# The weight sum S1 of each Strassen group: added by an accumulating DMA of GpSimd's queue instead of by VectorE

## The chip, the cores and the metric

The kernel runs on one core of a Trainium2 chip. The metric is the device time of one execution in microseconds (us). The engines are PE (TensorE, matrix products), DVE (VectorE), ACT (ScalarE), POOL (GpSimd) and SP (SyncE, which here only issues transfers). Every engine works through its own list of instructions in order and waits on semaphores for the others.

## The reference

One block of an encoder in float32, 1024 tokens of width 1024: two SwiGLU feed-forward layers around a token mixing stage.

```
h = h + 0.5 * swiglu_ffn(rmsnorm(h), ffn1_w_in, ffn1_w_out)
u = rmsnorm(h); proj = u @ w_in          # q, k, v, g_ret, p, gates
...                                       # retention, multi-scale pooling
merged = gate0 * (ret @ w_ret_up) + gate1 * (pool_out @ w_pool_up)
h = h + merged @ w_out
h = h + 0.5 * swiglu_ffn(rmsnorm(h), ffn2_w_in, ffn2_w_out)
return rmsnorm(h)

swiglu_ffn(x) = (silu(gate) * up) @ w_out,  [gate | up] = x @ w_in
```

The feed-forward width is 2816, and w_in has 7168 columns.

## The kernel before, in words

Activations are held transposed, channels on the partitions and tokens along the free dimension. Each product of a weight with activations is worked out in float32 from two parts of each operand, a rounded high part and the rest: `split` (L150 to L152) makes them, the high part by a cast on ACT (L151), the low part by a subtraction on DVE (L152), and `mm3` (L171 to L173) does three matmuls of 512 columns for each product.

The large weight matrices go through Strassen's scheme in Winograd's form: seven products of blocks instead of eight. One *group* is `strassen()` (L391): it takes two adjacent tiles of 128 output channels, wa and wb, each 128 x 1024, and cuts each in two halves of 512: L11 and L12 from wa, L21 and L22 from wb. The weight side of the scheme is S1 = L21 + L22, S2 = S1 − L11, S3 = L11 − L21, S4 = L12 − S2. `blocks()` in it loads wa to a tile `ra` and wb to `rb` (two loads of 512 KB on SP's queue, `load`, L134) and `combine()` (L403 to L405) makes each sum on DVE, one instruction of 128 x 512. In the order of the code S1 is made just ahead of S2, in the step of S2, and read again later, when the step of S1 splits it for its own product.

Each of the seven steps has a preparation (`prep_w`: sums, then the split) and a body (`b1` to `b7`: 12 matmuls on PE, then copies and evacuations). `b1` begins a bank for the sum b by copying the first product on ACT (L437, "a_b" from "a_a" in the profile); the next product of b goes onto that copy, so PE needs it. `Flow.run` calls the preparation of a step four steps (`LOOK`) ahead of its body. Background work (evacuating, scaling, storing of earlier groups) is added between bodies, some pieces a step (`flow.rate`). Evacuations marked `soon` get a high priority from the scheduler of the tile framework, which sets the order on each engine and puts in the waits.

Buffers come from pools: `raw` (4 tiles of 128 x 1024, for ra and rb), `wt` (5, split weights) and `c2` (8 tiles of 128 x 512; S1 to S4 and most intermediate values of an evacuation). A new tile in a pool waits until the last reader of the tile that it replaces is done.

79 groups use `strassen()`: 21 in the first feed-forward's input (names a1 to a21, one more, a0, is done plainly), 28 in the projections (v, t, g, p, q, k), 8 in the merge (ru0 to ru3 and wo0 to wo3), 22 in the second feed-forward's input (c0 to c21). In the feed-forwards gate tiles g and up tiles g + 11 take turns: a11, a1, a12, a2 and so on, and two groups that follow each other form a pair (a16 and a6, then a17 and a7). In most pairs the seventh product is shared: `third()` gives both groups' S4 terms from one product's worth of smaller ones, so a pair takes 13 products. When a gate tile and its up tile are done and the swish is taken, `w1`, `w2`, `w3` in `ffn_in` store the operands for the next stage: b, r, t and m, four stores on SP's queue (m is made by the subtraction at L669). The output products of the feed-forwards (`ffn_out`) have their own S1, S2, S3; the change does not touch those.

Of the kernel before, what the change touches and what calls it, by code (L numbers as in the profile page):

```python
# [15 lines left out]
ADD, SUB, MUL = ALU.add, ALU.subtract, ALU.mult  # L16
# [5 lines left out]
H = S // 2  # L22
# [67 lines left out]
def block_kernel(ctx: ExitStack, tc, x, x_tok, vecs, f1_in, f1_out, w_in, pool_w, w_ret, w_pool, w_o,  # L90
                 f2_in, f2_out, rope, decay, consts, out, out_tok):
    nc = tc.nc
# [21 lines left out]
    def raw(name):  # L114
        return sb.tile([P, S], F32, tag="raw", bufs=N_RAW, name=name)
# [7 lines left out]
    def c2(name):  # L123
        return sb.tile([P, H], F32, tag="c2", bufs=N_C2, name=name)

    def bank(name):
        return ps.tile([P, H], F32, tag="ps", name=name)

    def sum_bank(name):

        return ps.tile([P, H], F32, tag="sum", bufs=N_SUM, name=name)

    def load(dst, src):
        nc.sync.dma_start(dst, src)  # L134
# [4 lines left out]
    def half(t, j):  # L139
        return t[:, j * H : (j + 1) * H]  # L140
# [22 lines left out]
    def weights(src, name):  # L163
        w = wt(name)
        n = src.shape[-1] // P
        split(flat(w, 0, n), flat(w, 1, n), src)
        return w

    def mm3(dst, w, m, start, stop):

        mm(dst, w[0], m[0], start=start, stop=False, skip_group_check=True)  # L171
        mm(dst, w[0], m[1], start=False, stop=False, skip_group_check=True)  # L172
        mm(dst, w[1], m[0], start=False, stop=stop, skip_group_check=True)  # L173

    def parts(m, at=slice(None)):
        return m[:, 0, at], m[:, 1, at]
# [214 lines left out]
    def strassen(nx, wa, wb, name, evac, end, begin=None, shared=False):  # L391

        t = {}

        def blocks():
            ra, rb = raw(f"{name}ra"), raw(f"{name}rb")
            load(ra, wa)
            load(rb, wb)  # L400
            t.update(L11=half(ra, 0), L12=half(ra, 1), L21=half(rb, 0), L22=half(rb, 1))

        def combine(n, a, b, op):  # L403
            t[n] = c2(f"{name}{n}")
            tt(t[n], t[a], t[b], op)  # L405

        def prep_w(n):
            def go():
                if n == "L11":
                    blocks()  # L410
                elif n == "S2":
                    combine("S1", "L21", "L22", ADD)
                    combine("S2", "S1", "L11", SUB)
                elif n == "S3":
                    combine("S3", "L11", "L21", SUB)
                if n == "S4" or shared and n == "L22":
                    combine("S4", "L12", "S2", SUB)
                t["w", n] = weights(t[n], f"{name}w{n}")

            return go  # L420

        def prod(dst, w, m, start, stop):
            for i in range(4):
                mm3(t[dst], parts(t["w", w], i), parts(nx.operand(m, i)), start and i == 0, stop and i == 3)

        def u(n):
            t[n] = c2(f"{name}{n}")
            return t[n]

        def b1():  # L430
            if begin:
                begin()
            t["a"] = bank(f"{name}a")
            prod("a", "L11", "R11", True, False)
            t["b"] = sum_bank(f"{name}b")
            with soon():
                copy(t["b"], t["a"])  # L437

        def b6():
            prod("b", "S2", "T2", False, False)  # L440
            with soon():
                copy(u("v"), t["b"])

        def fourth():

            if "b5" in t and "p7" in t:
                with soon():
                    evac((1, 1), t["b"], t["p7"])

        def b5():  # L450
            prod("b", "S1", "T1", False, False)
            t["b5"] = True
            fourth()

        def b7():
            t["e"] = bank(f"{name}e")
            prod("e", "S3", "T3", True, False)
            with soon():
                copy(u("p7"), t["e"])
            fourth()  # L460

        def b2():
            prod("a", "L12", "R21", False, True)
            with soon():
                evac((0, 0), t["a"], None)

        def b3():
            prod("b", "S4", "R22", False, True)
            with soon():
                evac((0, 1), t["b"], None)  # L470

        def b4():
            prod("e", "L22", "T4", False, True)
            with soon():
                evac((1, 0), t["e"], t["v"])

        def last(f):
            def go():
                f()
                t["ends"] = t.get("ends", 0) + 1  # L480
                if t["ends"] == 2:
                    end()

            return go

        g = Group([(prep_w("L11"), b1), (prep_w("S2"), b6), (prep_w("S1"), b5), (prep_w("S3"), b7),
                   (prep_w("L12"), b2), (prep_w("S4"), last(b3)), (prep_w("L22"), last(b4))])
        g.t, g.name, g.third = t, name, last(lambda: evac((0, 1), t["b"], t.get("z")))
        return g
# [965 lines left out]
    class Last(Norm):  # L1455
# [58 lines left out]
        def end(self, part):  # L1514
            if part == 2:
                flow.add(self.finish)
                return
            tokens = (slice(H, S), slice(0, HD))[part]
            at = {}

            def stats():
                r = inverse_root(token_sums(self.ssq, range(tokens.start // P, tokens.stop // P), f"fin{part}"), D,
                                 f"fin{part}")
                at["b"] = spread(r, f"fin{part}")

            def scale(mt):
                t = self.tiles[mt][:, tokens]
                stt(t, t, vec[:, V_FINAL + mt : V_FINAL + mt + 1], at["b"], MUL, MUL)
                load(out[mt, :, tokens], t)

            flow.add(stats, *(lambda mt=mt: scale(mt) for mt in range(KT)))
            if part == 1:
                flow.add(*(lambda mt=mt: self.gain(mt) for mt in range(4)))
# [94 lines left out]
```

## Time and profile before

| | |
|---|---|
| median of 3 runs | 2176.23 us (2175.84 to 2177.58) |
| profiled execution | 2176.49 us |
| its span | 2174.3 us |
| mean granted clock | 0.998 |
| transfers | 311.96 MB, 143 GB/s over the span |

The page of the profile gives each engine's busy time, the chain of work that ended last, and groups of instructions. Names leave out buffer numbers: "a_S" is S1, S2, S3 or S4 of some a group, "a_rb" its rb tile, "a_wS" a split of such a sum. A row of a timeline has the start, the length, the engine (SPq is the queue of SP), the line, the operation, and in brackets the idle time ahead of it with what ended it. Lines of DMA issues end with the median time from issue to landing.

### The profile page before, as it was taken

The numbers are of one execution on the slowest core, as the hardware profiler recorded it, in microseconds if no ns is written. First come the engines' busy times: TensorE is split into PE (matmuls) and PEld (weight loads), VectorE is DVE, ScalarE is ACT, GpSimd is POOL, SyncE is SP. The second block draws the span as 40 slices with busy tenths as digits, with TensorE's granted clock in tenths as the row PEclk, the third lists the DMA queues.
The fourth block names the chain that finished last, engine by engine and source line by source line (L and its number), as shares of the span: only waits on it lengthen the run. The fifth ranks groups of instructions, "written<-read, shape, count | busy, mean of one in ns | idle before, by whom it ended". The sixth has DMA issues, their size and how long they took to land.

```text
span 2174.3 us, 29003 instructions
## 1 busy us (share of the span) xinstructions
PE 2163.3 (99%) x10556; PEld 1825.3 (84%) x10556; DVE 1786.0 (82%) x3068; ACT 1041.0 (48%) x1911; POOL 0.2 (0%) x4
## 2 busy tenths in 40 slices
PE   9999999999999999999999999999999999999998
PEld 7888888888888888888888998878888888888888
DVE  8797878888687687888887787799997878799774
ACT  8443434455554434444446663456634434344561
POOL 0000000000000000000000000000000000000000
PEclk9999999999999999999999999999999999999999
DMA  6233323596323332323345557524232322359522
GB/s 231 86 125 110 126 92 106 181 329 218 101 92 114 110 136 97 126 97 124 109 175 184 187 188 276 188 88 142 82 136 83 126 93 93 125 186 342 174 83 78
DMA packets 110448, 311.96 MB, mean 143 GB/s; under 512 B 12385, under 2 KB 13537, under 8 KB 110305
## 3 DMA queue, kind: packets, MB, share of 16 engines
q1 hardware_dynamic: 110304, 310.11, 41.4%
q8 instruction: 83, 1.36, 0.3%
q14 instruction: 61, 0.49, 0.1%
HBM read 219.36 MB, written 90.70 MB: 143 GB/s over the span
## 4 chain that ended last, share of the span: by engine, by line
PE 96%; DVE 2%; ACT 1%; DMA 0%; issue 0%; SPq 0%; DVEq 0%; ACTq 0%
PE c_b L171 2%; PE c_b L173 2%; PE c_b L172 2%; PE a_b L172 2%; PE a_b L171 2%; PE a_b L173 2%; PE c_e L171 2%; PE c_a L172 2%; PE c_a L171 2%; PE c_a L173 2%; PE c_e L173 2%; PE c_e L172 2%; PE a_a L172 2%; PE a_a L171 2%; PE a_e L172 2%; PE a_e L171 2%
## 5 line engine op out<-in xcount | busy, mean ns | idle before, releaser
L151 ACT CAST c_wS<-c_S 128x512 fp32r<-128x512 f32 x72 | 44.7, 621 | 74.9 <-DVE c_S L405 47.6
L172 PE MATMUL c_a<-n3R,c_wL 128*128 128x512 f32 x176 | 68.7, 390 | 0.0
L173 PE MATMUL c_a<-n3R,c_wL 128*128 128x512 f32 x176 | 68.5, 389 | 0.0
L172 PE MATMUL c_b<-n3T,c_wS 128*128 128x512 f32 x176 | 68.5, 389 | 0.0
L173 PE MATMUL c_b<-n3T,c_wS 128*128 128x512 f32 x176 | 68.5, 389 | 0.0
L171 PE MATMUL c_a<-n3R,c_wL 128*128 128x512 f32 x176 | 68.4, 390 | 0.0
L171 PE MATMUL c_b<-n3T,c_wS 128*128 128x512 f32 x176 | 68.1, 389 | 0.0
L151 ACT CAST a_wS<-a_S 128x512 fp32r<-128x512 f32 x68 | 42.1, 620 | 52.3 <-DVE a_S L405 30.4
L171 PE MATMUL a_a<-n1R,a_wL 128*128 128x512 f32 x168 | 65.5, 390 | 0.0
L172 PE MATMUL a_a<-n1R,a_wL 128*128 128x512 f32 x168 | 65.5, 390 | 0.0
L173 PE MATMUL a_a<-n1R,a_wL 128*128 128x512 f32 x168 | 65.4, 389 | 0.0
L171 PE MATMUL a_b<-n1T,a_wS 128*128 128x512 f32 x168 | 65.4, 389 | 0.0
L172 PE MATMUL a_b<-n1T,a_wS 128*128 128x512 f32 x168 | 65.4, 389 | 0.0
L173 PE MATMUL a_b<-n1T,a_wS 128*128 128x512 f32 x168 | 65.4, 389 | 0.0
L152 DVE TENSOR_TENSOR a_wS<-a_S,a_wS 128x512 fp32r<-128x512 f32 x68 | 46.4, 684 | 4.9 <-ACT a_wS L151 4.8
L152 DVE TENSOR_TENSOR c_wS<-c_S,c_wS 128x512 fp32r<-128x512 f32 x72 | 49.3, 685 | 1.2 <-ACT c_wS L151 1.0
L151 ACT CAST c_wL<-c_ra 128x512 fp32r<-128x512 f32 x44 | 27.1, 619 | 27.1 <-PE c_e L173 22.5
L151 ACT CAST a_wL<-a_ra 128x512 fp32r<-128x512 f32 x42 | 26.0, 622 | 27.1 <-PE a_e L173 22.4
L173 PEld LDWEIGHTS c_a<-n3R,c_wL 128*128 128x128 f32 x176 | 33.0, 188 | 6.9
L173 PEld LDWEIGHTS c_b<-n3T,c_wS 128*128 128x128 f32 x176 | 33.0, 188 | 6.9
L172 PEld LDWEIGHTS c_a<-n3R,c_wL 128*128 128x128 f32 x176 | 33.1, 188 | 6.8 <-DVE n3R L156 0.3
L171 PEld LDWEIGHTS c_b<-n3T,c_wS 128*128 128x128 f32 x176 | 33.0, 188 | 6.8
(3019 smaller groups left out, 7713.9 us busy)
## 6 DMA issues: line engine op xcount, KB each, us to landing
c_ra<-in_f_in SPq DMA_DIRECT2D x22, 512.0 KB, 3.6
c_rb<-in_f_in SPq DMA_DIRECT2D x22, 512.0 KB, 4.3
a_ra<-in_f_in SPq DMA_DIRECT2D x21, 512.0 KB, 4.1
a_rb<-in_f_in SPq DMA_DIRECT2D x21, 512.0 KB, 4.9
t<-au SPq DMA_DIRECT2D x11, 512.0 KB, 2.6
b<-an SPq DMA_DIRECT2D x11, 512.0 KB, 2.8
r<-au SPq DMA_DIRECT2D x11, 512.0 KB, 3.0
bra<-in_f_out SPq DMA_DIRECT2D x11, 512.0 KB, 6.2
```

The source lines that it names most:

```text
L151: copy(hi, src)
L152: tt(lo, src, hi.bitcast(F32), SUB)
L171: mm(dst, w[0], m[0], start=start, stop=False, skip_group_check=True)
L172: mm(dst, w[0], m[1], start=False, stop=False, skip_group_check=True)
L173: mm(dst, w[1], m[0], start=False, stop=stop, skip_group_check=True)
```

## The change

`blocks()` now takes S1's tile and fills it by two transfers: SP loads the first half of wb into it (256 KB), and GpSimd then issues a transfer of the second half with `accum_op=ADD` into the same tile. The line that made S1 on VectorE is gone. S1's tile of the c2 pool is thus taken in the preparation of L11, two steps earlier than before in the order of the feed-forwards, and each half of wb is read from HBM twice, once for rb and once for S1.

```diff
@@ blocks()
             ra, rb = raw(f"{name}ra"), raw(f"{name}rb")
             load(ra, wa)
             load(rb, wb)
+
+            t["S1"] = c2(f"{name}S1")
+            load(t["S1"], wb[:, :H])
+            nc.gpsimd.dma_start(t["S1"], wb[:, H:], accum_op=ADD)
             t.update(L11=half(ra, 0), L12=half(ra, 1), L21=half(rb, 0), L22=half(rb, 1))
@@ prep_w()
                 elif n == "S2":
-                    combine("S1", "L21", "L22", ADD)
                     combine("S2", "S1", "L11", SUB)
```

The lines of the program below it stand three or four further down. GpSimd's list, four memsets before, gets 79 transfers, one a group, in the order of the groups. VectorE's list has 2971 rows before and 2897 after; SP's has 738 and 818.

SP's queue in the first feed-forward input, where the stores of an earlier pair (t4, b4, r4, m4) meet the loads of the groups ahead. Before:

```order
L134 DMA t4_137<-au15_1944 128x1024
L134 DMA b4_148<-an4_2195 128x1024
L134 DMA r4_126<-au4_1741 128x1024
L134 DMA m4_159<-am4_2196 128x512
L134 DMA a17_ra_2407<-in_f1_in 128x1024
L134 DMA a17_rb_2408<-in_f1_in 128x1024
L134 DMA a7_ra_2549<-in_f1_in 128x1024
L134 DMA a7_rb_2550<-in_f1_in 128x1024
```

After, at the same place of SP's queue:

```order
L134 DMA a17_ra_2419<-in_f1_in 128x1024
L134 DMA t4_137<-au15_1956 128x1024
L134 DMA b4_148<-an4_2206 128x1024
L134 DMA r4_126<-au4_1749 128x1024
L134 DMA m4_159<-am4_2207 128x512
L134 DMA a6_S1_2241<-in_f1_in 128x512
L134 DMA a17_rb_2420<-in_f1_in 128x1024
L134 DMA a7_ra_2562<-in_f1_in 128x1024
L134 DMA a7_rb_2563<-in_f1_in 128x1024
L134 DMA a17_S1_2423<-in_f1_in 128x512
```

a6's S1 load stands behind the four stores, a17's behind the loads of a7; a17's ra has moved ahead of the stores.

VectorE at the same place, where the sums of a6 are made among the evacuations of a16 (ag16, au16) and the product of gate and up tiles of an earlier group (au5). Before:

```order
L405 TENSOR_TENSOR a6_S3_2249<-a6_ra_2226,a6_rb_2227 128x512
L647 TENSOR_TENSOR au5_2065<-ag5_2064,au5_2065 128x512 x2
L152 TENSOR_TENSOR a6_wS3_2251<-a6_S3_2249,a6_wS3_2251 128x512
L634 TENSOR_TENSOR ag16_2266<-a16_a_2180,n1rb_970 128x512
L405 TENSOR_TENSOR a6_S1_2270<-a6_rb_2227 128x512
L405 TENSOR_TENSOR a6_S2_2272<-a6_S1_2270,a6_ra_2226 128x512
L405 TENSOR_TENSOR a6_S4_2326<-a6_ra_2226,a6_S2_2272 128x512
L632 TENSOR_TENSOR au16_2267<-a16_b_2193,a16_p7_2221 128x512
L152 TENSOR_TENSOR a6_wS2_2274<-a6_S2_2272,a6_wS2_2274 128x512
```

After, at the same place of VectorE's list:

```order
L409 TENSOR_TENSOR a6_S3_2263<-a6_ra_2237,a6_rb_2238 128x512
L637 TENSOR_TENSOR ag16_2280<-a16_a_2191,n1rb_974 128x512
L152 TENSOR_TENSOR a6_wS3_2265<-a6_S3_2263,a6_wS3_2265 128x512
L635 TENSOR_TENSOR au16_2281<-a16_b_2204,a16_p7_2232 128x512
L641 TENSOR_TENSOR au16_2281<-au16_2281,n1rb_974 128x512
L409 TENSOR_TENSOR a6_S2_2284<-a6_S1_2241,a6_ra_2237 128x512
L409 TENSOR_TENSOR a6_S4_2338<-a6_ra_2237,a6_S2_2284 128x512
L635 TENSOR_TENSOR au16_2281<-a16_e_2219,a16_v_2259 128x512
L152 TENSOR_TENSOR a6_wS2_2286<-a6_S2_2284,a6_wS2_2286 128x512
```

The add of S1 is gone, and S2 now reads a tile that transfers fill; one evacuation of a16 has moved ahead of S2, and S4 and the low half of S2 stand behind it as before.

VectorE in the merge, from the step behind wo0's S2 to wo1's S2 (mgt, mgT and ru are operands of the next product and the tiles that they are made from; wo00 and wo10 are results). Before:

```order
L302 TENSOR_TENSOR mgt12_13450<-ru20_13069 128x512
L302 TENSOR_TENSOR mgt13_13456<-ru30_13104 128x512
L1423 TENSOR_TENSOR wo00_13431<-wo0a_13435,wo00_13431 128x512
L152 TENSOR_TENSOR wo0wS2_13428<-wo0S2_13426,wo0wS2_13428 128x512
L295 TENSOR_TENSOR ru20_13069<-ru21_13071,mgt12_13450 128x512
L295 TENSOR_TENSOR ru30_13104<-ru31_13106,mgt13_13456 128x512
L1423 TENSOR_TENSOR wo10_13469<-wo1a_13473,wo10_13469 128x512
L152 TENSOR_TENSOR mgT22_13453<-ru20_13069,mgT22_13453 128x512
L152 TENSOR_TENSOR mgT23_13459<-ru30_13104,mgT23_13459 128x512
L405 TENSOR_TENSOR wo1S1_13462<-wo1rb_13346 128x512
L295 TENSOR_TENSOR ru20_13069<-ru21_13071,ru20_13069 128x512
L405 TENSOR_TENSOR wo1S2_13464<-wo1S1_13462,wo1ra_13345 128x512
```

After, the same stretch:

```order
L302 TENSOR_TENSOR mgt12_13507<-ru20_13124 128x512
L302 TENSOR_TENSOR mgt13_13513<-ru30_13157 128x512
L152 TENSOR_TENSOR wo0wS2_13485<-wo0S2_13483,wo0wS2_13485 128x512
L1426 TENSOR_TENSOR wo00_13488<-wo0a_13492,wo00_13488 128x512
L295 TENSOR_TENSOR ru20_13124<-ru21_13126,mgt12_13507 128x512
L295 TENSOR_TENSOR ru30_13157<-ru31_13159,mgt13_13513 128x512
L409 TENSOR_TENSOR wo1S2_13519<-wo1S1_13405,wo1ra_13401 128x512
```

Besides wo1's S1, four steps that stood ahead of wo1's S2 now follow it.

## The prediction

> **What bounds the kernel now.** I read the page's busy shares and chain first, then the windows, and only then single engines.
>
> ```profile
> PE 2163.3 (99%) x10556; PEld 1825.3 (84%) x10556; DVE 1786.0 (82%) x3068; ACT 1041.0 (48%) x1911; POOL 0.2 (0%) x4
> ...
> q1 hardware_dynamic: 110304, 310.11, 41.4%
> ...
> PE 96%; DVE 2%; ACT 1%; DMA 0%; issue 0%; SPq 0%; DVEq 0%; ACTq 0%
> ```
>
> From the groups by line of DVE, those that read nothing but rb, which is S1's add alone, and from the windows a steady stretch and two of the merge (columns: length, busy time of PE, PEld, DVE, ACT, POOL, granted clock, DMA share, GB/s):
>
> ```profile
> L405 DVE TENSOR_TENSOR c_S<-c_rb 128x512 f32<-128x512 f32 x22 | 15.1, 685 | 0.0
> L405 DVE TENSOR_TENSOR a_S<-a_rb 128x512 f32<-128x512 f32 x21 | 14.4, 684 | 0.0
> ...
> 85.00:380.00 295.00, 295.00 (x1439) 250.01 (x1439) 254.49 (x439) 127.23 (x220) 0.00 (x0) 1.00 0.31 110
> 1455.00:1465.00 10.00, 9.62 (x42) 7.43 (x40) 9.96 (x18) 3.50 (x7) 0.00 (x0) 1.00 0.32 115
> 1465.00:1475.00 10.00, 8.32 (x28) 6.41 (x29) 9.45 (x16) 7.46 (x14) 0.00 (x0) 0.83 0.23 73
> ```
>
> TensorE is busy 99% of the span and carries 96% of the chain that ended last; VectorE has 2% of the chain, though it is busy 82%. The window 85 to 380 is the steady state of the first feed-forward stage: PE never stops, DVE is idle 295.00 − 254.49 = 40.5 us. So what the change takes from DVE there is worth nothing by itself. The two windows of the merge stage are the exception: DVE is busy 9.96 and 9.45 of 10 us, PE loses time, and the clock is 0.83.
>
> **What the change removes.** The rows of the two feed-forward inputs hold 22 and 21 S1 adds of 0.685 us; with 28 groups in the projections and 8 in the merge it is 79, so 79 × 0.685 = 54 us of DVE work go. Almost all of it lies under PE. The chain of waits, from 1457 on, shows where it does not:
>
> ```profile
> 1457.00 0.62 DVE wo0S L405
> ...
> 1463.74 0.60 DVE wo1S L405
> ```
>
> Both pieces are S1 adds (of wo0 and wo1), on a DVE chain without gaps. In PE's timeline that chain ends so:
>
> ```profile
> 1464.23 0.40 PE L173 MATMUL wo0b<-mgT,wo0wS 128*128 128x512 f32 x1
> 1466.25 0.50 PE L171 MATMUL wo1b<-mgT,wo1wS 128*128 128x512 f32 x1 [1.63 <-ACT wo1wS L151]
> 1466.59 0.39 PE L172 MATMUL wo1b<-mgT,wo1wS 128*128 128x512 f32 x1
> 1467.41 0.50 PE L173 MATMUL wo1b<-mgT,wo1wS 128*128 128x512 f32 x1 [0.42 <-DVE wo1wS L152]
> ...
> 1468.53 0.63 PE L173 MATMUL wo1b<-mgT,wo1wS 128*128 128x512 f32 x1
> 1468.96 0.63 PE L171 MATMUL wo1b<-mgT,wo1wS 128*128 128x512 f32 x1
> ```
>
> Undisturbed matmuls start 0.23 apart, as the two before the wait do in the steady state (the rows at 241.69 and 241.92 further down). So PE loses 2.02 − 0.23 = 1.8 us before 1466.25 and 0.82 − 0.23 = 0.6 us before 1467.41: 2.4 us. Behind that some eight matmuls start 0.43 apart instead of 0.23 (1468.53 to 1468.96), 8 × 0.2 = 1.6 us more; together about 4.0. The two adds alone are 0.62 + 0.60 = 1.2 us of that chain. The new order does a little more: between wo0's S2 and wo1's S2 twelve steps become seven, so wo1's S2 comes six steps of 0.60 = 3.6 us earlier, counting wo0's own S1. That covers the 2.4 us. What is late next is wo1's third operand: its low half comes only two adds, 1.2 us, earlier, behind the same full DVE, so I don't credit the slow matmuls. Term one: **−2.4 us**, between −1.2 and −4.0.
>
> **What it adds.** Per group a plain 256 KB load behind rb on SP's queue, a 256 KB accumulating transfer on GpSimd's queue that waits for that load, and a wait of DVE for it at S2. POOL does nothing else (0.2 us), so nothing is queued behind its waits but later accumulations, and those come in the order of the groups. DMA: 79 × 0.52 MB = 41 MB on 312, with q1's share at 41%: room enough. On SP, 79 more issues of about 0.4 us; SP sits idle for microseconds between the rows below.
>
> The wait is the real question, and the timelines around one such group price it: SP, then DVE, ACT and PE. The adds at 231.94 and 232.66 make a6's S1 and S2, the one at 254.91 a17's S1.
>
> ```profile
> 227.83 0.32 SPq L134 DMA_DIRECT2D m<-am  x1
> 228.24 0.40 SPq L134 DMA_DIRECT2D a_ra<-in_f_in  x1
> ...
> 241.26 0.33 SPq L134 DMA_DIRECT2D a_rb<-in_f_in  x1
> ```
>
> ```profile
> 227.11 0.69 DVE L669 TENSOR_TENSOR am<-au,au 128x512 f32<-128x512 f32 x1
> ...
> 231.94 0.68 DVE L405 TENSOR_TENSOR a_S<-a_rb 128x512 f32<-128x512 f32 x1
> 232.66 0.69 DVE L405 TENSOR_TENSOR a_S<-a_S,a_ra 128x512 f32<-128x512 f32 x1
> ...
> 254.91 0.69 DVE L405 TENSOR_TENSOR a_S<-a_rb 128x512 f32<-128x512 f32 x1
> ```
>
> ```profile
> 233.46 0.62 ACT L151 CAST a_wS<-a_S 128x512 fp32r<-128x512 f32 x1 [2.98 <-DVE a_S L405]
> 234.02 0.62 ACT L151 CAST a_wL<-a_ra 128x512 fp32r<-128x512 f32 x1
> 236.74 0.62 ACT L151 CAST a_wS<-a_S 128x512 fp32r<-128x512 f32 x1 [2.10 <-PE a_e L173]
> 239.40 0.57 ACT L437 COPY a_b<-a_a 128x512 f32<-128x512 f32 x1 [2.04 <-PE a_a L173]
> ```
>
> ```profile
> 220.13 0.40 PE L171 MATMUL a_a<-n1R,a_wL 128*128 128x512 f32 x1
> ...
> 241.69 0.39 PE L173 MATMUL a_e<-n1T,a_wS 128*128 128x512 f32 x1
> 241.92 0.39 PE L171 MATMUL a_b<-n1T,a_wS 128*128 128x512 f32 x1
> ...
> 257.83 0.40 PE L171 MATMUL a_a<-n1R,a_wL 128*128 128x512 f32 x1
> ```
>
> By the new order a6's S1 load stands directly behind the store m4 on SP. That store waits for the subtraction that ends at 227.11 + 0.69 = 227.80, so S1 is issued about where a_ra is now, at 228.24. DVE is ready for S2 at 231.94, once S1's add is gone: the two transfers have only **3.7 us** before DVE waits. For the first group of the next pair (a17) the S1 load stands behind a7's rb, issued at 241.26, so it goes out at about 241.7, and S2 can begin at 254.91: 13.2 us, enough.
>
> How long are two transfers? The nearest rows, with the median from issue to landing last:
>
> ```profile
> h<-wo SPq DMA_DIRECT2D x16, 256.0 KB, 2.0
> m<-am SPq DMA_DIRECT2D x11, 256.0 KB, 2.7
> v<-v SPq DMA_DIRECT2D x16, 256.0 KB, 4.0
> dL22a<-in_f_out SPq DMA_DIRECT2D x11, 256.0 KB, 4.6
> bacc<-in_x SPq DMA_DIRECT2D x8, 512.0 KB, 9.9
> ```
>
> The plain load is between 2.0 and 4.6; I take 4.0, from the row of a read into SBUF among other traffic. No accumulating transfer is in this trace. Its bounds are 2.0 (the fastest 256 KB) and 9.9 (the slowest 512 KB; an add has to read the tile as well as the new data, so twice the bytes). I take 5, nearest to the 256 KB reads, with 1 us for the second reading. S1 thus lands L = 9 us after issue, with ends 4.0 and 14.5, and DVE waits 9 − 3.7 = 5.3 us at S2 of such a group. The Trainium skill's page "DMA: Bandwidth & Descriptors" (Anatomy of one DMA, the GpSimd path) gives 2.0 us plus the bytes at 436 GB/s, 2.6 us for 256 KB; by it L would be 6.6 and the wait 2.9. No run here shows that path yet.
>
> Who pays for the wait? DVE behind S2: S4, an evacuation, the low halves. ACT, in order: the cast of S2 (0.11 after S2 ends), two more casts at a pitch of 0.56, then the copy a_b, which PE's product at 241.92 needs. With S2 starting at X the copy ends at X + 0.69 + 0.11 + 3 × 0.56 + 0.57 = X + 3.05, so PE loses nothing while X is under about 238.8, which is L under 238.8 − 228.24 = 10.56, say **10.5 us**. L = 9 leaves 1.5 us. DVE finds the 5.3 us in its slack: a pair of groups takes PE from 220.13 to 257.83, 37.7 us, so the window's 295 us hold 7.8 pairs, and its 40.5 us of DVE idle are 5.2 per pair, and 2 × 0.6 us of removed adds come on top. Term two: **0**, if L stays under 10.5; about +1 us per pair and us of L beyond.
>
> Sum: 2176.49 (profiled; its span is 2174.3, with 2.2 outside it) − 2.4 = 2174.1; against the median of 2176.23, 0.26 lower, 2173.8.
>
> **The rivals.** *S1 comes too late (slower).* The same chain with L over 10.5: the copy a_b waits, PE waits for it, once per pair; there are 10 + 14 + 11 = 35 pairs in the three stages. L = 11.5 gives +35, less 2.4: 2209; L = 12.2 gives 1.7 × 35 = 60: about 2234; the end 14.5 gives +140. For it: three further transfers of 512 KB (a17's rb, a7's ra and rb) share the engines with the accumulation, and some rows of 512 KB take 9.9 us. Against it: SP's own gaps, DMA share 0.31 in this window, and the projections and the second feed-forward have more room in the order, as several S1 loads there stand well ahead of their S2.
>
> *VectorE starves GpSimd (slower).* If the accumulation could only start while DVE pauses, tight groups would lose nothing, since DVE itself stops at S2 and so frees it: the load lands near 228.24 + 4.0 = 232.2, S2 stops DVE at 231.94. In a group such as a17, where DVE is busy for most of the time before 254.91, the accumulation could slip to the stop at S2, 5 us late, just ahead of evacuations that PE needs at once: up to 35 × 5 = +175, 2349. Against it: DVE has 14% idle in that window. The skill's page "SBUF — State Buffer" (Who interferes with whom) says that copies and tensor_scalar in VectorE's two-port modes keep GpSimd from writing descriptors, and that tensor_tensor seems not to. Nearly all DVE rows here are TENSOR_TENSOR. By that rule this rival is out; no run here shows it.
>
> *SP is held up (slower).* S1's buffer is claimed two steps earlier from the pool of eight. If its load waits in SP for a buffer, the next rb waits behind it, 5 to 10 us in a few early groups: about 2184.
>
> *More than the stall goes (faster).* If the merge also loses its slow matmuls (−4.0) and early waits of the other merge groups give another 0.7, it is 2171.5.
>
> *Nothing moves.* The merge stall finds another late operand at once: 2176.2.
>
> **How the numbers follow.** A measurement of this kernel can tell about 0.2%, 4.35 us, from no change, so the forecast of −2.4 counts as the same. Chances: forecast (−1.2 to −4.0) 0.46, nothing moves 0.08, S1 too late 0.28, starvation 0.04, SP 0.04, more than the stall 0.10. Faster 0.10, same 0.54, slower 0.36. The forecast alone would range from 2172.2 to 2175.0. The range starts at 2171.0, just under the faster case, and goes to 2236, L = 12.2 in all pairs; beyond that lie about 0.16, the upper half of the late case and starvation. The likeliest single value stays 2173.8.
>
> **What would show it.** Right: PE at 295 of 295 us in the same window; DVE total near 1786 − 54 = 1732; a wait of DVE for a DMA of 4 to 6 us at S2, once per pair, and with it L of 8 to 10 in the rows of DMA issues; no 1.6 us wait of PE before wo1b. Wrong: PE waiting for the copy a_b or for a cast of S2 in each pair (late S1); waits also at S2 of the roomy groups with an accumulation that starts only there (starvation); SP rows with an S1 load that waits for VectorE or PE (SP held up). A wait at S2 of under 1 us would mean that my 9 us for the pair is too long; one over 6.9 us, too short.

## The result, and the profile after

The changed kernel takes 2188.86 us (median of 5 runs, 2188.09 to 2192.55) beside 2177.03 us for the one before (5 runs): 1.0057 times as long, 95% interval 1.0044 to 1.007. It is 11.8 us slower. Its profiled execution has a span of 2186.4 us against 2174.3, at the same mean clock of 0.998.

From the page of the changed kernel, the rows that answer to those of before, and from its windows the steady stretch and the merge (the merge now stands some 9 us later, so a third window is added):

```profile
PE 2165.0 (99%) x10556; PEld 1824.5 (83%) x10556; DVE 1734.7 (79%) x2989; ACT 1038.4 (47%) x1911; POOL 69.2 (3%) x83
...
q1 hardware_dynamic: 121680, 330.82, 44.0%
q0 software_dynamic: 11376, 20.71, 6.0%
...
PE 88%; DVE 6%; DMA 3%; ACT 2%; issue 1%; SPq 0%; DVEq 0%; ACTq 0%; POOLq 0%
```

```profile
85.00:380.00 295.00, 292.17 (x1422) 246.61 (x1421) 243.78 (x427) 125.79 (x217) 13.04 (x15) 1.00 0.43 131
...
1455.00:1465.00 10.00, 10.00 (x46) 8.26 (x44) 10.00 (x18) 1.93 (x4) 1.76 (x2) 1.00 0.63 147
1465.00:1475.00 10.00, 10.00 (x46) 8.29 (x45) 10.00 (x17) 6.52 (x12) 0.00 (x0) 1.00 0.39 133
1475.00:1485.00 10.00, 9.54 (x39) 6.76 (x38) 10.00 (x18) 6.70 (x13) 0.00 (x0) 1.00 0.16 41
```

VectorE did lose its 51 us (1786.0 to 1734.7), and the merge did lose its stall: PE is busy 10.00, 10.00 and 9.54 where it was 9.62 and 8.32, at full clock. But DMA now has 3% of the chain that ended last, and VectorE 6%. What the transfers took, from the rows of DMA issues (last number: median us from issue to landing), is close to what was forecast:

```profile
c_S<-in_f_in SPq DMA_DIRECT2D x22, 256.0 KB, 4.1
c_S<-in_f_in POOLq DMA_DIRECT2D x22, 256.0 KB, 4.2
...
a_S<-in_f_in SPq DMA_DIRECT2D x21, 256.0 KB, 5.0
a_S<-in_f_in POOLq DMA_DIRECT2D x21, 256.0 KB, 4.0
```

Over all 79 groups S1 lands 9.5 us (median) after the first issue: 4.45 for the load, 0.66 until GpSimd has issued, 4.0 for the accumulation. The waits of DVE and of PE, each as total, number and longest, show two quite different things:

```profile
DVE c_S L409 <- DMA c_S<-in_f_in: 38.7, 12, 5.5
DVE a_S L409 <- DMA a_S<-in_f_in: 21.7, 11, 4.1
```

```profile
PE k3b L171 <- ACT g3wS L151: 2.7, 1, 2.7
PE a_x L171 <- DVE a_z L535: 1.6, 1, 1.6
PE a_e L171 <- ACT a_wS L151: 1.6, 1, 1.6
...
PE n10b L230 <- DVE n10dg L229: 1.2, 1, 1.2
PE t2b L171 <- ACT t2b L440: 1.0, 1, 1.0
```

VectorE waits for S1 some 60 us in the two feed-forward stages, and PE hardly notices: in the second one, with 38.7 us of such waits, it has no row among these. PE waits once at a time, at five or six places. The table sums PE's starts beyond the steady pitch (gaps of more than 0.32 us between starts, less 0.23), by stage, in us:

| stage (us of the span) | before | after | both halves by GpSimd (e8) | that, but not the first pair (e9) |
|---|---|---|---|---|
| beginning, 0 to 100 | 4.4 | 8.7 | 6.8 | 4.5 |
| first feed-forward, 100 to 650 | 0 | 1.7 | 0 | 0.1 |
| projections, 650 to 1150 | 1.0 | 6.9 | 1.0 | 1.0 |
| retention, 1150 to 1400 | 2.0 | 2.5 | 2.0 | 2.0 |
| merge and begin of the second, 1400 to 1650 | 5.9 | 3.5 | 2.7 | 3.7 |
| rest | 0.5 | 1.6 | 0.5 | 0.7 |
| sum | 13.8 | 24.9 | 13.0 | 12.0 |

That is 11.1 of the 12.1 us by which the spans differ: +4.3 at the beginning, +1.7 and +5.9 in the first feed-forward and the projections, −2.4 in the merge.

One of the places, followed back along the chain of waits in the changed kernel (DMA pieces run from issue to landing):

```profile
769.82 0.61 DVE k0wL L152
770.43 0.02 issue
770.44 0.33 SPq L134
...
770.87 5.35 DMA t2S<-in_w_in
...
776.88 3.90 DMA t2S<-in_w_in
780.78 0.02 issue
780.80 0.70 DVE t2S L409
...
783.15 0.59 ACT t2b L440
...
783.78 0.50 PE t2b L171
```

It starts with VectorE's split of k0. That step frees a raw buffer, for which SP has been waiting to issue the load of p1's rb (770.44). t2's S1 load stands right behind that load in SP's list, so it can't go before 770.87. Then come the two transfers, S2 on VectorE at 780.80, the casts on ACT in order, the copy t2b, and PE. From S2's start to PE's it is 2.98 us; the prediction had 3.05 for this chain. At g3, the costliest place, the chain begins the same way:

```profile
1107.11 0.62 DVE k3wL L152
...
1108.18 4.81 DMA g3S<-in_w_in
...
1113.66 5.58 DMA g3S<-in_w_in
...
1119.26 0.70 DVE g3S L409
```

Here PE waits for something else. VectorE's timeline has an evacuation right behind the stalled S2, and PE's product adds onto the bank that it empties:

```profile
1119.26 0.69 DVE L409 TENSOR_TENSOR g3S<-g3S,g3ra 128x512 f32<-128x512 f32 x1 [4.92 <-DMA g3S<-in_w_in]
1119.87 0.68 DVE L994 TENSOR_TENSOR k3B<-k3b,k3p 128x512 f32<-128x512 f32 x1
```

```profile
1120.70 0.61 PE L171 MATMUL k3b<-n2R,k3wS 128*128 128x512 f32 x1 [2.73 <-ACT g3wS L151]
```

The wait is put down to ACT's cast of g3's S2, which ended last. The product reads k3's operand, not g3's, and the bank k3b, which VectorE reads until 1120.55; the product's own waits are on VectorE and ACT. So the evacuation is the likelier one; both stand behind the same S2. Two runs below bear it out: in e6 and e8 this evacuation stands ahead of g3's S2 in VectorE's list, VectorE still waits 3.4 and 1.6 us for S1, and PE doesn't wait.

In SP's list of the changed kernel all four late groups stand directly behind the raw loads of a later group:

```
a13_ra a13_rb a2_S1
a5_ra  a5_rb  a15_S1
p1ra   p1rb   t2S1
       v2ra   g3S1
```

Theory A: the loss is that of single places where S1 comes late, a2, a15, t2 and g3, and the first pair, because its first load stands in SP's queue behind loads that wait for a raw buffer (at the beginning, because the transfer engines are full). Theory B: the added traffic delays other transfers. Theory C: the loss is spread over all pairs, or comes from the changed order on the engines.

### The profile page after: what moved, and what is told of

It is laid out like the page before. It is cut to its first block, busy times and chain, and to the rows that moved or that the text cites. A ratio compares the mean times of both kernels' runs of the same rounds, so it can differ in the third digit from the quotient of the medians.

```text
span 2186.4 us, 29303 instructions
## 1 busy us (share of the span) xinstructions
PE 2165.0 (99%) x10556; PEld 1824.5 (83%) x10556; DVE 1734.7 (79%) x2989; ACT 1038.4 (47%) x1911; POOL 69.2 (3%) x83
## 3 DMA queue, kind: packets, MB, share of 16 engines
q0 software_dynamic: 11376, 20.71, 6.0%
## 4 chain that ended last, share of the span: by engine, by line
PE 88%; DVE 6%; DMA 3%; ACT 2%; issue 1%; SPq 0%; DVEq 0%; ACTq 0%; POOLq 0%
PE c_b L171 2%; PE c_b L173 2%; PE c_b L172 2%; PE a_b L171 2%; PE a_b L173 2%; PE a_b L172 2%; PE c_e L171 2%; PE c_e L173 2%; PE c_e L172 2%; PE a_e L172 2%; PE a_e L171 2%; PE c_a L172 2%; PE c_a L173 2%; PE a_e L173 2%; PE a_a L171 2%; PE c_a L171 2%
## 5 line engine op out<-in xcount | busy, mean ns | idle before, releaser
L409 DVE TENSOR_TENSOR c_S<-c_S,c_ra 128x512 f32<-128x512 f32 x22 | 15.2, 690 | 38.7 <-DMA c_S<-in_f_in 38.7
```

## The experiments

Each run was timed beside the kernel before, and its ratio is to that time: 2175.71 (e1 to e4), 2176.07 (e5 to e8), 2176.29 (e9 to e11) and 2175.26 (e12).

**e1: S2 without S1.** In groups that have S3 already, S2 is made from it.

```diff
                 elif n == "S2":
-                    combine("S2", "S1", "L11", SUB)
+                    if "S3" in t:
+                        combine("S2", "L22", "S3", SUB)
+                    else:
+                        combine("S2", "S1", "L11", SUB)
```

> In every group that makes S3 before S2 (all but the first pair of each of the three large stages and the merge) S2 is now made as L22 - S3, which is the same sum, so that S2 no longer reads S1; S1 still comes by the two transfers, and traffic and queues stay as in the changed kernel. Theory A (four places pay for the late S1 at S2: a2, a15, t2 and g3, 1.35 + 1.69 + 1.19 + 2.89 us and 1.6 us of slow clock behind the last, 8.7 us together): 2180, with waits of DVE for S1's transfers at S2 gone. Theory B (the 79 more loads and 41 MB delay other transfers): 2187 to 2190 as in the changed kernel, since the traffic is the same.

Measured: 2178.49, ratio to before 1.0012 (1.0003 to 1.0021). With the same traffic and the same transfers 9 of the 12 us are gone, and PE's gaps come to 16.7 us, 8.2 less than in the changed kernel. Theory B falls as the main cause: traffic, SP's extra issues and all else together come to a net 2.8 us. Two waits are still there that the kernel before doesn't have, 1.7 us at 47 and 0.9 us at 62; e3 comes back to them.

**e2: the traffic alone.** VectorE adds as before; the two transfers go to a tile of its own (not printed: the constant `zero` of the warm-up moves to the same single buffer).

```diff
-            t["S1"] = c2(f"{name}S1")
-            load(t["S1"], wb[:, :H])
-            nc.gpsimd.dma_start(t["S1"], wb[:, H:], accum_op=ADD)
+            x = sb.tile([P, H], F32, tag="sx", bufs=1, name=f"{name}SX")
+            load(x, wb[:, :H])
+            nc.gpsimd.dma_start(x, wb[:, H:], accum_op=ADD)
```

> VectorE makes S1 as in the kernel before, and the load and the accumulating transfer of each group go to a tile of their own that nothing reads. Theory A: nothing waits, so the time of the kernel before, 2177, within 2. Theory B: most of the 12 us stays, 2185 or more.

Measured: 2310.84, ratio 1.0612 (1.0598 to 1.0627). Neither theory said so, and the run answers another question than the one put. With one buffer and nothing to hold them to their place, the loads were ordered far ahead; each waits in SP's queue for the accumulation before it, and the loads that matter wait behind it. SP's timeline at 200 us, in the first feed-forward, where the projections' names (t0, q0) should not appear at all:

```profile
211.08 0.33 SPq L134 DMA_DIRECT2D t0SX<-in_w_in  x1
218.28 0.33 SPq L134 DMA_DIRECT2D q0SX<-in_w_in  x1
225.53 0.33 SPq L134 DMA_DIRECT2D t1SX<-in_w_in  x1
225.95 0.38 SPq L134 DMA_DIRECT2D t<-au  x1
```

Such a load goes out every 7.2 us, and the stores wait meanwhile. On the traffic it is inconclusive; on an in-order queue it is a lesson.

**e3: the first half alone.**

```diff
             load(t["S1"], wb[:, :H])
-            nc.gpsimd.dma_start(t["S1"], wb[:, H:], accum_op=ADD)
```

> The accumulating transfer is left out, so S1 is L21 alone and the output is another; the plain load and DVE's wait for it stay. S1 lands 4 to 6.5 us after its issue instead of 8.2 to 11. Theory A: the waits at a2, a15, t2 and g3 go, 2180. Theory B: half of the extra traffic stays, 2183 to 2186. A third reading, that the change of the order on each engine costs the 12 us by itself: 2188.

Measured: 2176.81, ratio 1.0004 (0.9995 to 1.0013). Without the second transfer S1 is early enough at the four places, and PE's waits there are gone. At the beginning one stays. The first pair's S1 now lands 6.4 and 7.6 us after its issue at 15.65 and 17.68, at 22.0 and 25.3, and S2 reads it more than 8 us later; yet PE waits at 47.0 as it did at 46.8 in the changed kernel:

```profile
30.72 0.69 DVE L408 TENSOR_TENSOR a_S<-a_S,a_ra 128x512 f32<-128x512 f32 x1
33.79 0.69 DVE L408 TENSOR_TENSOR a_S<-a_S,a_ra 128x512 f32<-128x512 f32 x1
```

```profile
47.00 0.50 PE L171 MATMUL a_e<-n1T,a_wS 128*128 128x512 f32 x1 [1.75 <-ACT a_wS L151]
```

So this wait is not a late S1. It comes with the changed order: on ACT, in the kernel before and then in the changed one, passes over an input tile (xs) have changed places with the cast that PE waits for:

```profile
42.35 1.14 ACT L151 CAST a_wS<-a_S 128x512 fp32r<-128x512 f32 x2
...
44.39 1.06 ACT L929 ACTIVATE xs<-xs 128x1024 f32<-128x1024 f32 x1
```

```profile
38.99 1.06 ACT L932 ACTIVATE xs<-xs 128x1024 f32<-128x1024 f32 x1
...
46.12 1.14 ACT L151 CAST a_wS<-a_S 128x512 fp32r<-128x512 f32 x2
```

Up to 100 us PE's gaps come to 7.5 us in e3 against 4.4 before, and in the merge to 2.7 against 5.9: the order costs some 3 us in one place and gains as much in the other, so the total shows nothing. Of the readings in the expectation only A's direction is left, and it expected 3 us too much.

**e4: two accumulations.**

```diff
             nc.gpsimd.dma_start(t["S1"], wb[:, H:], accum_op=ADD)
+            nc.gpsimd.dma_start(t["S1"], wb[:, H:], accum_op=ADD)
```

> The accumulating transfer is made twice, one behind the other, so S1 is L21 + 2 L22 and the output is another; S1 lands about 4.7 us later, 14.5 us after its issue. If the bound of 10.5 us holds that the prediction worked out for a steady pair, each of some 30 to 35 pairs now loses about 4 us: 2300 to 2330. If the steady pairs have more room than that and only single places pay, 4.7 us at each of the four places and a few more: 2205 to 2220.

Measured: 2402.69, ratio 1.1041 (1.1021 to 1.1061): 214 us more than the changed kernel for 4.7 us more of latency. So the steady pairs do have a limit, and it lies between 9.5 and 14 us, where the prediction put it. The expectation undershot the price because of the clock: the mean granted clock is 0.974, which over 2402 us is at most 62 us lost. PE's gaps grew by 207 us; without those 62 it is 145, and 35 pairs times 4 us would be 140. But the sum is right with half of it by another chain. PE waits 60 times for more than 1 us, 157 us together: 32 of these (77 us) are at the bank that the copy a_b begins, as the prediction has it, and 22 (57 us) at the shared product, for a sum (L536 here) that VectorE makes one or two steps behind a waiting S2. The prediction's chain doesn't have that one.

**e5: four groups by VectorE.** Here and below a condition on the name decides between the two transfers and VectorE's add.

```diff
+            if name not in ("a2_", "a15_", "t2", "g3"):
                 t["S1"] = c2(f"{name}S1")
...
                 elif n == "S2":
+                    if "S1" not in t:
+                        combine("S1", "L21", "L22", ADD)
                     combine("S2", "S1", "L11", SUB)
```

> S1 is made by VectorE again in four of the 79 groups alone, a2, a15, t2 and g3, the places where the chain of the changed kernel shows TensorE waiting behind a late S1. Theory A (few places pay): 8.7 of the 11.8 us go, 3 us above the kernel before, about 2179. Rival (the loss is spread over the pairs, and these four only show it first): 1 or 2 us go, 2186, and the waits come back at neighbouring groups.

Measured: 2179.34, ratio 1.0015 (1.0006 to 1.0024), as theory A said to within 0.4 us. Four groups of 79 give back 8.5 of 11.8 us. The others go on waiting, at no cost to PE; the waits of its VectorE, and its window 85 to 380:

```profile
DVE c_S L410 <- DMA c_S<-in_f_in: 38.4, 11, 5.5
DVE a_S L410 <- DMA a_S<-in_f_in: 14.6, 8, 3.8
```

```profile
85.00:380.00 295.00, 295.00 (x1437) 249.47 (x1436) 244.85 (x423) 126.77 (x219) 12.18 (x14) 1.00 0.42 130
```

The loss spread over the pairs, theory C's first half, falls. Of its second half, the order, the wait at the beginning is left (1.9 us at 47.8).

**e6: the same four by transfers, all others by VectorE** (`name in (...)`).

> The complement: only a2, a15, t2 and g3 get S1 by the two transfers, all other groups by VectorE. Theory A: most of the 8.7 us, 2182 to 2185, unless SP's queue, now without the other loads, issues these four earlier. Rival (spread): 2177.

Measured: 2179.74, ratio 1.0018 (1.0009 to 1.0027): 3.7 us, less than half of what theory A said. PE waits at a2 (1.7) and at t2 (1.1) as in the changed kernel, and not at a15 and g3. Their S1 loads still stand behind the same raw loads, and S1 still takes 9.7 and 11.0 us, but VectorE now waits 3.4 us at g3 instead of 4.9. The traces show why. At g3 VectorE's list has the evacuation of k3's bank (1110.86) ahead of S2 (1115.59) here, so nothing that PE needs stands behind the wait. At a15 S1 lands at 178.06 and S2 comes only at 181.37, without a wait. So a late S1 costs time only where the order puts something for PE behind it.

**e7: the merge alone** (`name[:2] in ("ru", "wo")`).

> Only the eight groups of the merge get S1 by the two transfers. By the gaps of TensorE the changed kernel loses 2.9 us less than the one before in that stage, and nothing else is changed here: 2173 beside 2176. If the gain there hangs on the changed order of the stages before it, 2176.

Measured: 2174.89, ratio 0.9995 (0.9987 to 1.0004), which is the time of before. PE's gap sum is 12.7 against 13.8: the 1.8 us stall ahead of wo1b is gone, and a new one of 1.2 us has come at wo3's first product. In this order more than about a microsecond is not to be had there.

**e8: both halves by GpSimd's queue.**

```diff
-            load(t["S1"], wb[:, :H])
+            nc.gpsimd.dma_start(t["S1"], wb[:, :H])
             nc.gpsimd.dma_start(t["S1"], wb[:, H:], accum_op=ADD)
```

> The first half of S1 is loaded by GpSimd's queue too, so that it no longer stands behind the stores and the rb loads on SP; it goes out as soon as its tile is free. The two transfers take as long as before (8 to 10 us). Theory A: S1 lands some microseconds earlier at a2, a15, t2 and g3, the waits there shrink, 2178 to 2182. If the lateness comes from the tile that is freed late, and not from SP's queue, nothing changes: 2188.

Measured: 2176.79, ratio 1.0006 (0.9997 to 1.0014): no difference from before any more. All 79 groups use transfers, with the same 41 MB. At t2, in GpSimd's timeline and then VectorE's:

```profile
764.12 0.58 POOL L403 DMA_DIRECT2D t2S<-in_w_in  x1 [22.93 <-DVE k0wS L152]
767.50 0.87 POOL L404 DMA_DIRECT2D t2S<-in_w_in  x1 [2.79 <-DMA t2S<-in_w_in]
```

```profile
773.77 0.69 DVE L409 TENSOR_TENSOR t2S<-t2S,t2ra 128x512 f32<-128x512 f32 x1 [0.84 <-DMA t2S<-in_w_in]
```

The first transfer goes out at 764.12 instead of 770.87, as soon as its tile is free, and S2 waits 0.84 us instead of 2.76. By then the changed kernel is 3.65 us later in its whole timeline (the same matmul in both), so 3.1 us of the 6.75 are a true gain. For all four places, in us:

| group | first issue, changed | first issue, e8 | timeline later by | so earlier by | L, changed | L, e8 |
|---|---|---|---|---|---|---|
| a2 | 75.78 | 69.51 | 0.4 | 5.9 | 9.05 | 7.13 |
| a15 | 174.81 | 167.83 | 1.8 | 5.2 | 11.15 | 8.26 |
| t2 | 770.87 | 764.12 | 3.65 | 3.1 | 9.91 | 9.62 |
| g3 | 1108.18 | 1101.86 | 5.0 | 1.3 | 11.06 | 11.07 |

L is the time from the first issue to the second landing. At a2 and a15 the transfers are also 1.9 and 2.9 us shorter; over all groups the median L falls from 9.5 to 8.7 (the plain half from 4.45 to 3.0, the accumulation up from 4.0 to 5.05). At g3 the evacuation has moved ahead of S2 besides. So e8 shows that the load's place in SP's queue makes S1 late. Only at t2 is it the later start almost alone; elsewhere the length and the order change with it, and the run doesn't separate them.

**e9: that, but for the first pair** (`name not in ("a11_", "a1_")` around e8's lines).

> Both halves of S1 by GpSimd's queue, as in the run before, but for the first pair of groups, a11 and a1, where VectorE adds. Theory A: no S1 is late, the merge keeps its gain of 2.9 us, and the beginning is that of the kernel before: 2173 to 2174 beside 2176, so slightly ahead of both. If the gain of the merge is given back elsewhere: 2176.

Measured: 2174.92, ratio 0.9994 (0.9985 to 1.0003). The span (2172.5 against 2174.3) and the gap sum (12.0 against 13.8) are the lowest here, but the times can't tell it from before: the merge's gain is partly given back in the 50 us behind it.

**e10: the second half without the add.**

```diff
-            nc.gpsimd.dma_start(t["S1"], wb[:, H:], accum_op=ADD)
+            nc.gpsimd.dma_start(t["S1"], wb[:, H:])
```

> As the changed kernel, but GpSimd's transfer only copies instead of adding, so S1 is L22 and the output is another. It prices the add: if adding costs about 1 us of the 4.0 us from issue to landing, as the prediction reckoned for the second reading, a landing takes 3.0 us and the kernel 2182; if the add is free, 4.0 us and 2188.

Measured: 2180.94, ratio 1.0023 (1.0012 to 1.0033). Its rows of DMA issues and queues:

```profile
c_S<-in_f_in POOLq DMA_DIRECT2D x22, 256.0 KB, 2.9
...
a_S<-in_f_in POOLq DMA_DIRECT2D x21, 256.0 KB, 2.8
```

```profile
q0 software_dynamic: 6320, 20.71, 3.1%
```

Adding costs 1.1 us of the 4.0 from issue to landing, the 1 us of the estimate. For the same 20.71 MB the adding queue has 11376 packets and 6.0% of the engines' time, the copying one 6320 and 3.1%. One microsecond less per group is worth 7 of the 12 us, since S1 misses its limits by 1 to 3 us at only a few places. The Trainium skill's page "DMA: Bandwidth & Descriptors" (Anatomy of one DMA) gives 2.0 us plus the bytes at 436 GB/s for a transfer of GpSimd, by estimate 2.6 us for 256 KB. The 2.9 us of the copy are near it, the 4.0 of the add are not.

**e11: g3 alone by VectorE** (`name != "g3"`).

> S1 of g3 alone by VectorE. Theory A with a clock term: the wait of 2.9 us ahead of k3's product goes, and so do the slow matmuls behind it, 1.6 us: 4.5 us less than the changed kernel, 2184.4, at a granted clock without a half-rate stretch at that place. If the slow matmuls do not hang on the wait: 2.9 us less, 2186.

Measured: 2185.35, ratio 1.0043 (1.0029 to 1.0057); PE's wait at k3 and the slow matmuls behind it are gone. The time lies between the two expectations and can't tell them apart: PE's 1.7 us at a15 are gone as well, though a15 still has its transfers (S1 takes 9.0 us there instead of 11.15), and new gaps of up to 0.9 us have come between 1540 and 1640. e12 speaks against the tie between wait and clock that was put in the expectation.

**e12: the first pair by VectorE** (`name not in ("a11_", "a1_")` around the lines of the change).

> The changed kernel with S1 of the first pair alone, a11 and a1, by VectorE. There the two transfers take 15.1 us from issue to the second landing, while the transfer engines are busy all the time (share 1.05 in the window from 10 to 20), and TensorE waits 1.7 us at 46.8 and 1.0 us at 61.2 behind operands that VectorE makes late. Theory A, now with the beginning as a further late place: both waits go, 2.8 us less than the changed kernel, 2186. Rival (another order of the instructions at the beginning): they stay, 2189.

Measured: 2184.59, ratio 1.0044 (1.003 to 1.0057). The gaps up to 100 us fall from 8.7 to 5.6; the waits at 46.8 and 61.2 are gone, the one behind a2 stays. That doesn't prove S1 late there, since the order at the beginning is that of before again, too. By e3 it is the order, the rival in the expectation, for the wait at 46.8. The one at 61.2 goes back along the chain to the load of a raw tile (a12's rb), issued at 53.31 when VectorE had freed its buffer, and not to S1.

At the same time PE's wait at k3 is now 3.2 us, longer than in the changed kernel (2.9), yet no slow matmuls follow. The clock records of the traces tell why. In each of the 14 traces the granted clock changes only at whole multiples of 3.413 us from the trace's first clock record. On this grid, the window of the wait and the one behind it in the changed kernel, then the two over which e12's wait lies (the clock is the third number from the end):

```profile
1117.46:1120.87 3.41, 0.68 (x4) 0.29 (x3) 1.61 (x3) 0.81 (x2) 0.00 (x0) 1.00 0.27 47
1120.87:1124.28 3.41, 3.41 (x9) 2.64 (x9) 3.41 (x7) 0.33 (x1) 0.00 (x0) 0.50 0.00 0
```

```profile
1111.72:1115.13 3.41, 1.62 (x8) 1.00 (x6) 0.15 (x1) 0.00 (x0) 0.00 (x0) 1.00 0.55 102
1115.13:1118.54 3.41, 2.12 (x9) 1.80 (x10) 3.41 (x6) 1.14 (x2) 0.00 (x0) 1.00 0.00 0
```

In the changed kernel PE is idle for 0.80 of one window, and the next has half rate. In e12 the wait falls across a border, 0.52 of one window and 0.38 of the next, and full clock stays. So the 1.6 us of slow clock were not a fixed companion of the wait at g3.

## Why the prediction was wrong

It forecast 2173.8, no measurable change, and gave 0.28 to "S1 comes too late". S1 did come too late, and the kernel is 11.8 us slower, but not as that rival has it, once per pair with L over 10.5: L is 9.5 us in the median, and four groups of 79 pay most of it. The forecast has the wrong sign; that the time lies inside the stated range, which reached up for that rival, is luck.

- **Term one, the merge, was right.** −2.4 was forecast; PE's gaps between 1450 and 1500 fell from 4.25 to 1.40, the slow matmuls included. What is late next is also the one named: the third product's low half, a wait of 0.59 us at wo1e. That the slow matmuls would stay was wrong; they went with the stall. It did not show in the total, and alone (e7) it is worth about a microsecond.
- **The length of the two transfers was right.** L was forecast as 9 (4.0 and 5) and measured as 9.5 (4.45, 0.66 and 4.0); the add's own 1 us was measured as 1.1. The wake-up of GpSimd between the two was left out, and the accumulation taken a little too long.
- **The steady pair was right, with the wait too large.** It would keep DVE waiting and PE not: e5 shows 295.00 of 295 us for PE. The wait at such a group was forecast as 5.3 us and is 2.6 at its longest between 196 and 262 (two of them, 4.3 us in all, in the waits of that window; in the second feed-forward the mean is 3.2 and the longest 5.5), since VectorE gets to S2 later than reckoned: two steps of an evacuation moved ahead of S2, and one of them waits for PE. The limit is real as well (e4), though half of what lies beyond it is lost at a sum of the shared product, and not at the copy.
- **The step that failed is "Term two: 0, if L stays under 10.5".** The limit was worked out at one group, and L as one number, and both were used for all 79. Measured, L runs from 7.4 to 15.1 us; at a15 and g3 it is over 10.5 itself. And four groups have lower limits. From L, and PE's wait in the changed kernel taken off it:

| group | L, us | PE's wait, us | so PE's limit for L, us |
|---|---|---|---|
| a2 | 9.05 | 1.35 | 7.7 |
| a15 | 11.15 | 1.69 | 9.5 |
| t2 | 9.91 | 1.19 | 8.7 |
| g3 | 11.06 | 2.89 | 8.2 |

These limits hold for this kernel's order alone: g3 has L = 11.0 in e6, and a15 has 10.0 in e12, without a wait of PE.

- **Two things make these limits lower.** The sentence that the projections "have more room in the order" looked at VectorE's need of S2, and not at what stands behind S2 there: at g3 an evacuation and at a15 a sum of the shared product (L535), both of which PE waits for, sit one or two steps behind it with no ACT chain in between, and behind a2 a normalization's step. And the S1 load is issued late, behind raw loads that wait for a buffer. The rival "SP is held up" had the queue right and the direction wrong: not rb behind S1, but S1 behind the rb of a later group. It got 0.04.
- **The beginning was left out.** The waits at 46.8 and 61.2 cost 2.8 us. The first pair's S1 takes 15.1 us there, with DMA at a share of 1.05 between 10 and 20 us, but e3 has the first of these waits with S1 early: it goes with the new order on VectorE and ACT. The second goes back to a raw load whose buffer VectorE frees late.
- **Starvation of GpSimd was rightly ruled out.** Accumulations land 4.0 us after issue with VectorE busy 79% of the span, and the shortest takes 3.5. That agrees with the rule of the Trainium skill's page "SBUF — State Buffer" (Who interferes with whom) on tensor_tensor.
- A slip in the working: beyond 2236 lie half of the 0.28 and the 0.04 of starvation, which is 0.18 and not 0.16. Nothing hangs on it.

What stays open: how much of e8's gain is the earlier start, the shorter transfers and the order; why the order at the beginning changed as it did; and the microsecond or two between 1500 and 1550 that come and go between these kernels.

## What to carry to other kernels

A wait that is hidden in the steady state is priced by its worst places, not by its median. List for every instance when the result is issued, when it is needed, and what stands behind the waiting step: the same late S1 cost PE 2.9 us at g3 with an evacuation behind it, and nothing with the evacuation ahead (e6). Look first at the ends of loops and the beginning. A load's latency begins when its queue gets to it. In a queue that works in order, a transfer put behind one that waits for a buffer starts when that buffer is free, and moving it to another queue (e8) took away the whole loss. A change also moves steps that it doesn't touch, so compare the order of each engine's list before blaming the new wait (e3). Work taken from an engine with slack buys nothing, so there is little to gain against such a risk.

## What the runs showed of the hardware

- An accumulating transfer of 256 KB lands 4.0 us after issue, a copying one on the same queue 2.9, with nearly twice the packets and twice the busy time of the transfer engines for the add.
- The same plain load of 256 KB lands 4.45 us after issue (median) behind the raw loads of SP's queue in the changed kernel, and 3.0 us from GpSimd's queue in e8.
- After some waits of PE the granted clock drops to one half for 3.41 us, always at whole multiples of 3.413 us from the trace's first clock record. Over the windows of this grid in all 14 traces, each of the 38 that ran at full clock and in which PE idled for more than 0.56 was followed by one at half rate, and of those at full clock with less than 0.45 none was; between the two both occur. The kernel before has 0.60 (1464.40 to 1467.81), the changed kernel 0.80. The Trainium skill's page "TensorE: Matmul & The Clock Gate" (Part 1) has a window of 3413 ns that runs free of the kernel and grants half rate after an idle one. The window agrees; but it needn't be all idle here. In e4 the stretches at half rate make up 123 us, at most 62 us lost.
